# Other groups of experts in a mixture-of-experts block: the first alone, then fours, the last three together; and one expert load three units later

## The chip, the cores and the metric

The kernel runs on one core of a Trainium2 chip. The metric is the device time of one execution in microseconds. Profiles are of one execution; the engines are PE (TensorE matmuls), PEld (its weight loads), DVE (VectorE), ACT (ScalarE), POOL (GpSimd) and SP (SyncE, which here only issues DMAs).

## The reference

512 tokens of width 1024, all float32. A mixer (convolution branch, attention branch, two gates) is followed by a sparse block: each token picks one of 8 groups and two of the group's 8 experts.

```python
u  = rmsnorm(x);  proj = u @ w_in                    # conv B, C, x | q, k, v | two gates
y_conv = (cb * dwconv3(cc * cx)) @ w_conv_out
y_attn = attention(rope(norm(q)), rope(norm(k)), v) @ w_attn_out   # softmax over 512 keys, 8 heads
h  = x + (sigmoid(gc) * y_conv + sigmoid(ga) * y_attn) @ w_o
# experts: g = argmax of 8 group logits, then the top 2 of the 8 experts in g, weights pg * softmax
ys = (silu(xs @ w1[e]) * (xs @ w3[e])) @ w2[e]       # for each of the 64 experts on its tokens
out = h + sum over a token's two experts of weight * ys
```

Each expert has w1 and w3 of 1024x512 and w2 of 512x1024: three arrays of 2 MB, 403 MB for all.

## The kernel before, in words

**The mixer** is a list of units, run in order. A unit is one projection of 128 columns, 24 matmuls (`proj`), with a tile of weights `raw` (0.5 MB) that SP loads one unit ahead. ACT casts `raw` to `wh`, DVE subtracts to get `wl`, the two parts in which a float32 weight is multiplied. `raw`, `wh` and `wl` have two buffers each. PE's outputs are named after the unit: `o_q`, `o_cc`, `o_cx`, `o_cb` while the heads' attention goes on (`s`, `tp_p`, `o_pv`), then `o_g` for the gates and `o_yc` for the convolution's output in turn, eight of each, then `o_g`, `o_ya` and `o_o`. The softmax's rows `p` live in slot `s5`.

**Expert weights** have places of their own: w1 and w3 of expert e in one of three wide slots, used in turn; w2 of expert e in one of four slots named in `order = [5, 2, 6, 7]`. Slot `s5` takes w2 of expert 0. All of these loads are issued by SP, in program order from the gates on (`late`), so a load whose slot is still in use holds up every load behind it in SP's queue. In the profile they are all `w<-in_w`. Nine are issued within the mixer, the others after it, each as soon as its slot is free.

**Experts.** For each expert e (32 places for tokens, `CAP`): `o_x` gathers its tokens by a matmul with a 0/1 matrix `pR`, which DVE transposes into `X`; `h` is its hidden layer (32 steps for w1 and w3 together); ACT and DVE make `gt` from it; `y` is its output, which ACT copies into a quarter of `Y`, 32 rows. Four experts share a `Y`, a matrix `p0` (from `slots_of`, with a row of places for each expert) and its weighted transpose `S`. After the fourth, `combine` spreads all four to the tokens: eight matmuls `o_c` of 128x512, each added to `acc` by DVE. A float32 matmul stands as two records in the trace. The groups are 0 to 3, 4 to 7, and so on to 60 to 63.

**The end.** Of the last group, experts 60 and 61 are spread by `combine_two` (eight `o_c` that read 64 rows), placed between the two halves of `h` of expert 62 and around it. Experts 62 and 63 share two banks for `y`; `last_scatter` makes their matrix `S_last` and the weights `w_last`. `finish_last` first copies half of `acc` into four PSUM banks by an identity matmul (`o_k`), then runs expert 63 and goes through four column pieces: `y` of a piece; ACT and DVE weigh it as two parts `y_last`; eight matmuls spread it into `o_c` (two token tiles) and onto `o_k` (the other two); DVE adds the first to `acc`, ACT copies the second; SP and ACT write the result. The last w2 comes in four pieces.

The order of PE's instructions is that of a scheduler, except where `pin` fixes it. An overflow loop behind the end runs for experts with more than 32 tokens; its instructions stand behind the last store.

Of the kernel before, what the change touches and what calls it, by code (L numbers as in the profile page):

```python
# [46 lines left out]
def block_kernel(ctx, tc, x, norm1_g, w_in, conv_w, q_norm_g, k_norm_g, w_conv_out,  # L47
# [49 lines left out]

    pa, psx, pt = ring((0, 1, 2, 3)), ring((4, 5)), ring((6, 7))

    def mm(o, l, r, start, stop):  # L100
        return TE.matmul(o, l, r, start=start, stop=stop)

    xt = cst.tile([P, NT, D], F32, name="xt")

# [575 lines left out]
        unit(lambda: fn(*args))  # L680

    unit(lambda: late.append(True))
    load_unit(load_output, 0)
    for k in range(NK):
        gate_unit("gc", 2, C_GC, k)
        yc_unit(k)
    for k in range(NK):
        gate_unit("ga", 6, C_GA, k)
        if k in (1, 4):
            load_unit(load_in, 0, k // 4)  # L690
# [199 lines left out]
    def scatter_banks(pwv):  # L890
        tp = pt("tp_s")
        tpv = tp.rearrange("p (k c) -> p k c", k=4)
        for t in range(NT):
            TE.transpose(tpv[:, t, :], pwv[:, t, :], ident)
        return tpv

    def scatter_matrix(pwv):
# [13 lines left out]
    def combine(S, Y, first=False):  # L911
        for t in range(NT):
            for n in range(2):
                combine_at(S, Y, t, n, first)

    def slots_of(posm, gq):
        p0 = mp.tile(shp, F32, tag="p0", name="p0")
        es = slice(4 * gq, 4 * gq + 4)
        for t in range(NT):
            V.tensor_tensor(p0[:, t], posm[:, t, es, None].to_broadcast(shp[:1] + shp[2:]),  # L920
                            io32[:, None, :].to_broadcast(shp[:1] + shp[2:]), op=OP.is_equal)
        return p0

    def weigh(p0, gq):
        es = slice(4 * gq, 4 * gq + 4)
# [10 lines left out]
    def hidden(X, w, meanwhile=None, take=None, between=None):  # L936
        h = (take or psx)("h")
        hv = h[:, 0:2 * P].rearrange("p (i c) -> p i c", i=2)

        for part in (slice(0, 1), slice(1, 2)) if take else (slice(0, 2),):  # L940
            if part.start and between:
                between()
            for k in range(NK):
                for q in range(4):
                    i = mm(hv[32 * q:32 * q + 32, part], X[:, k, :], w[:, part, k, q * P:(q + 1) * P],
                           k == 0, k == NK - 1)
                    if take:
                        pin(i)
        sg = mp.tile([P, P], F32, tag="sg", name="sg", bufs=2)
        A.activation(sg, h[:, 0:P], AF.Silu)  # L950

# [6 lines left out]
        o = meanwhile() if meanwhile else None  # L958
        return gt, o

    def expert(el, X, ws, Y, meanwhile):
        w, c = ws
        gt, o = hidden(X, w, meanwhile=meanwhile)
# [11 lines left out]
    def combine_two(S, Y, ts):  # L975

        for t in ts:
            for n in range(2):
                nsl = slice(n * 512, (n + 1) * 512)
                o = pa("o_c")  # L980
                pin(mm(o, S[:2 * CAP, t, :], Y[:2 * CAP, nsl], True, True))
                V.tensor_tensor(acc_at(t, n), o, acc_at(t, n), op=OP.add)

    def last_scatter():


        p = slot(order[3], [P, NT, 4, CAP], F32, "p_last")
        for t in range(NT):
            for i in range(2):
                e = NE - 2 + i  # L990
                half = [P, 2, CAP]
                V.tensor_tensor(p[:, t, 2 * i:2 * i + 2], posm[:, t, e:e + 1, None].to_broadcast(half),
                                io32[:, None, :].to_broadcast(half), op=OP.is_equal)
        pv = p.rearrange("p t e s -> p t (e s)")
        S = wide_slot((NE - 1) % 3, [P, NT, P], F32R, "S_last")
        A.copy(S, scatter_banks(pv))
        o = pt("w_last")
        for t in range(NT):
            mm(o[:, 0:2], pv[:, t, :], W[:, t, NE - 2:NE], t == 0, t == NT - 1)
        ws = mp.tile([P, 1], F32, name="w_last")  # L1000
        for i in range(2):
            A.copy(ws[64 * i:64 * i + 64, :], o[64 * i:64 * i + 64, i:i + 1])
        return S, ws

    PIECES = list(zip(CUTS, CUTS[1:]))

    def last_two(i, gt, c, y, qs):

        for q in qs:
            c0, c1 = PIECES[q]  # L1010
            for k in range(4):
                r = 64 * i + 32 * (k % 2)
                pin(mm(y[q // 2][r:r + 32, 256 * (q % 2):256 * (q % 2) + 256], gt[:, k * CAP:(k + 1) * CAP], c[k][:, c0:c1],
                       k < 2, k > 1))

    def finish_last(X, ws, y, Sl, wl):

        w, c = ws
        kept = [bank(q, "o_k") for q in range(4)]
        for q, (c0, c1) in enumerate(PIECES):  # L1020
            pin(mm(kept[q].rearrange("p (t c) -> p t c", t=2), ident, acc[:, 2:4, c0:c1], True, False))
        gt, _ = hidden(X, w, take=lambda nm: bank(7, nm))
        hl = slot(order[0], [P, 4, 2, 256], F32R, "y_last")
        ov = out.rearrange("(t p) d -> p t d", p=P)

        def out_of(q):
            last_two(1, gt, c, y, (q,))
            yq = y[q // 2][:, 256 * (q % 2):256 * (q % 2) + 256]
            pin(A.activation(hl[:, q, 0, :], yq, AF.Copy, scale=wl))
            pin(V.scalar_tensor_tensor(hl[:, q, 1, :], yq, wl, hl[:, q, 0, :].bitcast(F32), op0=OP.mult, op1=OP.subtract))  # L1030

        def spread(q):
            c0, c1 = PIECES[q]
            o = bank(6 + q % 2, "o_c")
            for t in range(NT):
                d = (o if t < 2 else kept[q])[:, 256 * (t % 2):256 * (t % 2) + 256]
                pin(mm(d, Sl[:, t, :], hl[:, q, 0, :], t < 2, False))
                pin(mm(d, Sl[:, t, :], hl[:, q, 1, :], False, t != 2))
            for h, src in enumerate((o, kept[q])):
# [65 lines left out]
    for e in range(NE):  # L1105
        if e >= 3:
            load_hidden(e)
            for i in [e + 2] if e < NE - 5 else [e] if e > NE - 4 else []:
                load_output(i)
        if e == 0:  # L1110
            X = X0
        elif e % 4 == 0:
            S = scatter_matrix(weigh(p0, e // 4))
        elif e % 4 == 3 and e < NE - 1:
            p0 = slots_of(posm, e // 4 + 1)
            gathers = prepare_gather(p0, G)
        if e % 4 == 0:
            Y = mp.tile([P, D], F32, tag="Y", name="Y", bufs=2)
        ws = w13.pop(e), wout.pop(e)
        if e == NE - 1:  # L1120
            finish_last(X, ws, y2, Sl, wl)
            break
        if e == NE - 2:

            combine_two(S, Y, (0,))
            gt, _ = hidden(X, ws[0], take=lambda nm: bank(7, nm), between=lambda: combine_two(S, Y, (1,)))
            X = gathered(gathers[3]())
            combine_two(S, Y, (2, 3))
            y2 = [bank(4 + i, "y") for i in range(2)]
            last_two(0, gt, ws[1], y2, range(4))  # L1130
            continue
        X = expert(e % 4, X, ws, Y, gathers[(e + 1) % 4] if e else None)
        if e == NE - 3:
            Sl, wl = last_scatter()
        if e == 0:
            posm, W = finish_routing()
            p0 = slots_of(posm, 0)
            gathers = prepare_gather(p0, V)
            X = gathered(gathers[1]())
            S = scatter_matrix(weigh(p0, 0))  # L1140
        if e == 3:
            acc = mp.tile([P, NT, D], F32, tag="acc", name="acc")
        if e % 4 == 3:
            combine(S, Y, e == 3)
        if e == 7:
            ov_base, ov_tab = overflow_table()
    overflow((wide_slot(0, [P, 2, NK, FE], F32, "ov13"), slot(order[1], [P, 4, D], F32, "ov2")))


# [30 lines left out]
```

## Time and profile before

| | us |
|---|---|
| runs: median (lowest to highest) of 3 | 1464.15 (1463.63 to 1465.65) |
| the profiled execution | 1464.65 |
| its span, first to last instruction | 1462.9 |
| PE busy | 1202.2 (82%) |
| DVE busy | 478.3 (33%) |
| ACT busy | 345.9 (24%) |
| POOL busy | 82.6 (6%) |
| DMA moved | 449.20 MB, 426 GB/s in the slices in which it is full |

Busy times are sums over the span; matmuls overlap, so a busy PE is not PE at its peak. In the page's slices a digit is the busy share of a fortieth of the span in tenths. The chain of waits is followed back from the last instruction: each piece is the work that the next one waited for. A DMA's "time to landing" runs from its issue to the last byte's signal.

### The profile page before, as it was taken

How to read it: one execution, taken by the hardware profiler on the slowest of the kernel's cores; microseconds unless marked ns; L12 is line 12 of the kernel's file. 1: busy time of each engine (PE TensorE's matmuls, PEld its weight loads, DVE VectorE, ACT ScalarE, POOL GpSimd, SP SyncE). 2: the span in 40 equal slices, each digit the busy share in tenths (PEclk: the TensorE clock that was granted, in tenths of full speed). 3: DMA queues.
4: the chain of work that ended last, by engine and by line, in shares of the span. 5: the costliest groups of instructions: out<-in, count | busy, mean ns of one | idle time of the engine just before them, and what ended most of it. 6: DMA issues, size and time to landing. Idle time of an engine off the chain costs nothing.

```text
span 1462.9 us, 25305 instructions
## 1 busy us (share of the span) xinstructions
PE 1202.2 (82%) x11186; PEld 797.2 (54%) x11186; DVE 478.3 (33%) x945; ACT 345.9 (24%) x715; POOL 82.6 (6%) x124
## 2 busy tenths in 40 slices
PE   9999999999999989687585775866857759577597
PEld 7888888778888866343342343433423334343354
DVE  5666665522234343122131221321202212122032
ACT  4444443422232242111111111111111111111121
POOL 1200000000002010000000000000000000000000
PEclk9999999999999999899898998988989899899799
DMA  6222222233645659999999999999999999999994
GB/s 167 76 82 64 68 73 73 93 105 90 208 153 180 265 224 425 426 426 426 427 424 427 426 427 426 426 425 426 426 426 425 427 424 426 428 425 426 426 415 153
DMA packets 110593, 449.20 MB, mean 307 GB/s; under 512 B 11537, under 2 KB 84241, under 8 KB 86034
## 3 DMA queue, kind: packets, MB, share of 16 engines
q1 hardware_dynamic: 110208, 447.29, 75.8%
q8 instruction: 89, 1.46, 0.4%
q10 hardware_dynamic: 274, 0.27, 0.1%
q14 instruction: 22, 0.18, 0.0%
HBM read 445.44 MB, written 2.10 MB: 306 GB/s over the span
## 4 chain that ended last, share of the span: by engine, by line
PE 63%; DMA 31%; ACT 2%; issue 1%; DVE 1%; SPq 1%; POOL 0%; POOLq 0%; ACTq 0%
DMA w<-in_w 31%; PE h L61 11%; PE o_c L61 8%; PE o_g L61 6%; PE y L61 5%; PE o_x L61 3%; PE o_yc L61 3%; PE o_cc L61 3%; PE o_q L61 3%; PE o_cb L61 3%; PE o_ya L61 3%; PE o_o L61 3%; PE o_cx L61 3%; PE s L61 2%; PE o_pv L61 1%
## 5 line engine op out<-in xcount | busy, mean ns | idle before, releaser
L61 PE MATMUL h<-w,X 128*32 128x256 f32 (+1 forms) x4224 | 296.4, 438 | 167.3 <-DMA w<-in_w 166.3
L61 PEld LDWEIGHTS h<-w,X 128*32 128x32 f32 x4224 | 163.5, 127 | 288.8 <-issue 234.7
L61 PE MATMUL y<-w,gt 128*32 128x256 f32 x2048 | 127.7, 381 | 61.4 <-issue 39.9
L61 DVE TENSOR_TENSOR wl<-raw,wh 128x1024 fp32r<-128x1024 f32 x76 | 99.6, 1310 | 132.9 <-ACT wh L61 128.2
L61 PE MATMUL o_x<-xt,pR 128*32 128x256 f32 x2048 | 133.3, 380 | 2.2 <-DVE pR L61 2.2
L61 PEld LDWEIGHTS y<-w,gt 128*32 128x32 f32 x2048 | 70.5, 109 | 115.7 <-issue 52.5
L61 DVE STREAM_TRANSPOSE X<-xs 128x256 f32<-128x256 f32 x64 | 28.4, 444 | 319.6 <-PE h L61 237.5
L61 ACT COPY Y<-y 32x256 f32<-32x256 f32 x248 | 89.9, 363 | 176.7 <-PE y L61 174.4
L61 ACT CAST wh<-raw 128x1024 fp32r<-128x1024 f32 x76 | 80.6, 1060 | 200.3 <-PE o_g L61 64.4
L61 PE MATMUL o_c<-Y,S 128*128 128x512 f32 (+1 forms) x256 | 114.9, 600 | 12.9 <-ACT Y L61 12.9
L61 ACT ACTIVATE sg<-h 128x128 f32<-128x128 f32 x64 | 17.7, 277 | 436.0 <-PE h L61 436.0
L61 DVE TENSOR_TENSOR sp<-h,sg 128x128 f32<-128x128 f32 x64 | 23.0, 360 | 273.0 <-ACT sg L61 273.0
L61 DVE TENSOR_TENSOR acc<-o_c,acc 128x512 f32<-128x512 f32 x124 | 85.8, 692 | 80.0 <-PE o_c L61 79.8
L61 PEld LDWEIGHTS o_x<-xt,pR 128*32 128x32 f32 x2048 | 73.1, 110 | 55.3 <-DVE acc L61 9.9
L61 PEld LDWEIGHTS o_c<-Y,S 128*128 128x128 f32 (+1 forms) x256 | 47.0, 189 | 73.4 <-issue 44.6
L61 PE MATMUL o_g<-u,wh 128*128 128x512 f32 x256 | 80.5, 395 | 0.0
L61 POOL TENSOR_TENSOR pR<-p,rstd 128x512 f32<-128x512 f32 x15 | 15.6, 1043 | 714.3 <-PE o_x L61 671.3
L61 PEld LDWEIGHTS o_g<-u,wh 128*128 128x128 f32 x256 | 48.1, 188 | 11.1
L61 PE MATMUL o_g<-u,wl 128*128 128x512 f32 x128 | 50.5, 394 | 0.0
L61 PE MATMUL o_o<-wh,m 128*128 128x512 f32 x128 | 40.8, 399 | 0.0
L61 PE MATMUL o_q<-u,wh 128*128 128x512 f32 x128 | 40.3, 396 | 0.0
L61 PE MATMUL o_cc<-u,wh 128*128 128x512 f32 x128 | 40.2, 395 | 0.0
(229 smaller groups left out, 1432.4 us busy)
## 6 DMA issues: line engine op xcount, KB each, us to landing
w<-in_w SPq DMA_DIRECT2D x191, 2048.0 KB, 29.4
raw<-in_w_in SPq DMA_DIRECT2D x52, 512.0 KB, 3.8
raw<-in_w_conv_out SPq DMA_DIRECT2D x8, 512.0 KB, 4.1
raw<-in_w_attn_out SPq DMA_DIRECT2D x8, 512.0 KB, 4.1
raw<-in_w_o SPq DMA_DIRECT2D x8, 512.0 KB, 4.8
xt<-in_x SPq DMA_DIRECT2D x4, 512.0 KB, 6.3
w<-in_w SPq DMA_DIRECT2D x4, 512.0 KB, 30.5
out<-acc SPq DMA_DIRECT2D x7, 256.0 KB, 2.3
```

The costliest lines, as they stand in the source:

```text
L61: i = call(*args, **kwargs)
```

## The change

Two things are edited. In the mixer, the load of expert 0's w2 moves from ahead of the first gate to behind the third pair of gate and convolution output. In the experts, the groups become: expert 0 alone, with a matrix of its own (`slots_first`) and a spreading of its own at expert 4 (`combine_first`); 1 to 4, 5 to 8, up to 57 to 60; and 61 to 63, which are spread together at the end. `combine_two` and `last_two` go.

```diff
     unit(lambda: late.append(True))
-    load_unit(load_output, 0)
     for k in range(NK):
         gate_unit("gc", 2, C_GC, k)
         yc_unit(k)
+        if k == 2:
+            load_unit(load_output, 0)
```

Groups: the matrix of group `gq` starts at expert 4 gq + 1; the last has experts 61, 62, 63, 63.

```diff
-        es = slice(4 * gq, 4 * gq + 4)
+        e0, strips = 4 * gq + 1, [slice(0, 4)] if gq < NE // 4 - 1 else [slice(0, 3), slice(2, 3)]
...
+    def combine_first(p, Y):
+        tp = pt("tp_s").rearrange("p (k c) -> p k c", k=4)
+        for t in range(NT):
+            TE.transpose(tp[:CAP, t, :], p[:, t, :], ident)
+        S = mp.tile([P, NT, P], F32, tag="S", name="S", bufs=1)
+        A.copy(S[:CAP], tp[:CAP])
+        for t in range(NT):
             for n in range(2):
                 o = pa("o_c")
-                pin(mm(o, S[:2 * CAP, t, :], Y[:2 * CAP, nsl], True, True))
+                mm(o, S[:CAP, t, :], Y[:CAP, n * 512:(n + 1) * 512], True, True)
                 V.tensor_tensor(acc_at(t, n), o, acc_at(t, n), op=OP.add)
```

The end: 61 and 62 are weighed in one piece beside expert 63's hidden layer, and only the last column piece keeps its `o_k`; in the other three DVE adds both halves. From expert 60 on PE's order is fixed as written (`tail`), and `h` of 62 and 63 is done in two halves, w1 and then w3 (`apart`).

```diff
+    def times_weight(hl, rows_, qs, src, wl):
+        A.activation(hl[rows_, qs, 0, :], src, AF.Copy, scale=wl[rows_])
+        V.scalar_tensor_tensor(hl[rows_, qs, 1, :], src, wl[rows_], hl[rows_, qs, 0, :].bitcast(F32),
+                               op0=OP.mult, op1=OP.subtract)
...
-        kept = [bank(q, "o_k") for q in range(4)]
-        for q, (c0, c1) in enumerate(PIECES):
-            pin(mm(kept[q].rearrange("p (t c) -> p t c", t=2), ident, acc[:, 2:4, c0:c1], True, False))
-        gt, _ = hidden(X, w, take=lambda nm: bank(7, nm))
+        times_weight(hl, slice(0, 64), slice(0, 4), Y[0:64].rearrange("p (q c) -> p q c", q=4), wl)
+        kept = bank(0, "o_k")
+        mm(kept.rearrange("p (t c) -> p t c", t=2), ident, acc[:, 2:4, PIECES[3][0]:], True, False)
+        gt, _ = hidden(X, w, take=lambda nm: bank(5, nm), apart=True)
...
-                if h:
-                    pin(A.copy(d, sv))
+                if h and q == 3:
+                    A.copy(d, sv)
                 else:
-                    pin(V.tensor_tensor(d, sv, d, op=OP.add))
+                    V.tensor_tensor(d, sv, d, op=OP.add)
```

How the instructions stand. First SP's queue where the convolution's output units begin; `raw<-in_w_in` are the projections and gates, `w_0` is w2 of expert 0 (the number behind a name counts tiles), and the lines of the difference are marked - for before and + for now.

```order
 L61 DMA raw<-in_w_in 128x8x128 x33
-L61 DMA w_0_2396<-in_w 128x4096
 L61 DMA raw<-in_w_conv_out 128x8x128
 L61 DMA raw<-in_w_in 128x8x128
...
 L61 DMA raw<-in_w_conv_out 128x8x128
 L61 DMA raw<-in_w_in 128x8x128
+L61 DMA w_0_2589<-in_w 128x4096
 L61 DMA raw<-in_w_conv_out 128x8x128
```

The load goes past six raw loads. On ACT, at the same place, the casts of those raw tiles:

```order
 L61 ACTIVATE p,m<-s,m,r 128x512 x2
+L61 CAST wh<-raw 128x1024
 L61 CAST cbH<-f 128x512
 L61 CAST O<-o_pv 128x512
 L61 CAST pp<-tp_p 128x4x128 x4
 L61 CAST O<-o_pv 128x512
+L61 CAST wh<-raw 128x1024
 L61 ACT_TABLE_LOAD
 L61 ACTIVATE gc<-o_g 128x512
-L61 CAST wh<-raw 128x1024 x4
+L61 CAST wh<-raw 128x1024 x2
```

Two casts that stood behind the first gate now stand ahead of it, the first of them ahead of `cbH`. PE's order in the mixer is the same in both kernels.

PE at experts 3 to 5, before:

```order
L61 MATMUL y<-w_3_3831,gt 32x256 x16
L61 MATMUL tp_s<-identr,p_4241 128x128 x4
L61 MATMUL o_c<-Y,S 128x512 x8
L61 MATMUL h<-w_4_4355,X 32x256 x32
L61 MATMUL o_x<-xt,pR 32x256 x16
L61 MATMUL y<-w_4_3829,gt 32x256 x16
L61 MATMUL o_x<-xt,pR 32x256 x41
L61 MATMUL h<-w_5_4454,X 32x256 x32
```

and now:

```order
L61 MATMUL y<-w_3_3831,gt 32x256 x16
L61 MATMUL o_x<-xt,pR 32x256 x13
L61 MATMUL h<-w_4_4328,X 32x256 x32
L61 MATMUL o_x<-xt,pR 32x256 x3
L61 MATMUL tp_s<-identr,p_first 32x128 x4
L61 MATMUL tp_s<-identr,p_4333 128x128 x4
L61 MATMUL y<-w_4_3829,gt 32x256 x16
L61 MATMUL o_c<-Y,S 128x512 x16
L61 MATMUL h<-w_5_4477,X 32x256 x32
```

The eight `o_c` ahead of `h` of expert 4 are gone, and sixteen stand ahead of `h` of expert 5. PE at the end, from expert 59's `y`, before:

```order
L61 MATMUL y<-w_59_9573,gt 32x256 x16
L61 MATMUL o_c<-Y,S 128x512 x8
L61 MATMUL h<-w_60_9860,X 32x256 x32
...
L61 MATMUL y<-w_61_9960,gt 32x256 x16
L61 MATMUL o_c<-Y,S 128x512 x2
...
L61 MATMUL o_c<-Y,S 128x512 x3
L61 MATMUL h<-w_62_10068,X 32x128 x32
L61 MATMUL o_c<-Y,S 128x512
L61 MATMUL y<-w_62_10071,gt 32x256 x16
L61 MATMUL o_k<-acc,identr 128x512 x4
L61 MATMUL h<-w_63_10208,X 32x128 x64
```

and now:

```order
L61 MATMUL y<-w_59_9596,gt 32x256 x16
L61 MATMUL h<-w_60_9864,X 32x256 x32
L61 MATMUL o_x<-xt,pR 32x256 x16
L61 MATMUL y<-w_60_9695,gt 32x256 x16
L61 MATMUL o_c<-Y,S 128x512 x8
L61 MATMUL h<-w_61_9984,X 32x256 x32
...
L61 MATMUL h<-w_62_10089,X 32x128 x64
L61 MATMUL o_x<-xt,pR 32x256 x16
L61 MATMUL y<-w_62_10092,gt 32x256 x16
L61 MATMUL o_k<-acc,identr 128x512
L61 MATMUL h<-w_63_10208,X 32x128 x64
```

The full `o_c` moved behind `y` of expert 60; the eight `o_c` of `combine_two` and three `o_k` are gone from between `y` of 60 and `h` of 63.

More of the change, by code (lines that the diff above doesn't have):

```diff
@@ L98, in block_kernel @@
     pa, psx, pt = ring((0, 1, 2, 3)), ring((4, 5)), ring((6, 7))
+    tail = []
     def mm(o, l, r, start, stop):
-        return TE.matmul(o, l, r, start=start, stop=stop)
+        i = TE.matmul(o, l, r, start=start, stop=stop)
+        return pin(i) if tail else i
     xt = cst.tile([P, NT, D], F32, name="xt")
@@ L893, in scatter_banks @@
         for t in range(NT):
-            TE.transpose(tpv[:, t, :], pwv[:, t, :], ident)
+            i = TE.transpose(tpv[:, t, :], pwv[:, t, :], ident)
+            if tail:
+                pin(i)
         return tpv
@@ L917, in slots_of @@
         p0 = mp.tile(shp, F32, tag="p0", name="p0")
-        es = slice(4 * gq, 4 * gq + 4)
+        e0, strips = 4 * gq + 1, [slice(0, 4)] if gq < NE // 4 - 1 else [slice(0, 3), slice(2, 3)]
         for t in range(NT):
-            V.tensor_tensor(p0[:, t], posm[:, t, es, None].to_broadcast(shp[:1] + shp[2:]),
-                            io32[:, None, :].to_broadcast(shp[:1] + shp[2:]), op=OP.is_equal)
+            for i, st in enumerate(strips):
+                some = [P, st.stop - st.start, CAP]
+                V.tensor_tensor(p0[:, t, st.start + i:st.stop + i],
+                                posm[:, t, e0 + st.start:e0 + st.stop, None].to_broadcast(some),
+                                io32[:, None, :].to_broadcast(some), op=OP.is_equal)
         return p0
     def weigh(p0, gq):
-        es = slice(4 * gq, 4 * gq + 4)
+        es = slice(4 * gq + 1, 4 * gq + 5)
         for t in range(NT):
@@ L934, in prepare_gather, with hidden @@
         return [lambda el=el: gather_expert(pR[:, :, el * CAP:(el + 1) * CAP]) for el in range(4)]
-    def hidden(X, w, meanwhile=None, take=None, between=None):
+    def hidden(X, w, meanwhile=None, take=None, apart=False):
         h = (take or psx)("h")
         hv = h[:, 0:2 * P].rearrange("p (i c) -> p i c", i=2)
-        for part in (slice(0, 1), slice(1, 2)) if take else (slice(0, 2),):
-            if part.start and between:
-                between()
+        for part in (slice(0, 1), slice(1, 2)) if apart else (slice(0, 2),):
             for k in range(NK):
                 for q in range(4):
[L945 to L948, printed above, removed]
+                    mm(hv[32 * q:32 * q + 32, part], X[:, k, :], w[:, part, k, q * P:(q + 1) * P],
+                       k == 0, k == NK - 1)
         sg = mp.tile([P, P], F32, tag="sg", name="sg", bufs=2)
@@ L959, in hidden, with expert @@
         return gt, o
-    def expert(el, X, ws, Y, meanwhile):
+    def expert(el, X, ws, Y, meanwhile, apart=False):
         w, c = ws
-        gt, o = hidden(X, w, meanwhile=meanwhile)
+        gt, o = hidden(X, w, meanwhile=meanwhile, apart=apart)
         X = gathered(o) if meanwhile else None
@@ L973, in expert, with slots_first, last_scatter @@
         return X
-    def combine_two(S, Y, ts):
-        for t in ts:
+    def slots_first():
+        p = mp.tile([P, NT, CAP], F32, tag="pR", name="p_first", bufs=2)
+        some = [P, NT, CAP]
+        V.tensor_tensor(p, posm[:, :, 0:1].to_broadcast(some), io32[:, None, :].to_broadcast(some), op=OP.is_equal)
+        G.tensor_tensor(p, p, W[:, :, 0:1].to_broadcast(some), op=OP.mult)
+        return p
+    def combine_first(p, Y):
[5 more added lines that the diff above has]
+        for t in range(NT):
             for n in range(2):
-                nsl = slice(n * 512, (n + 1) * 512)
                 o = pa("o_c")
-                pin(mm(o, S[:2 * CAP, t, :], Y[:2 * CAP, nsl], True, True))
+                mm(o, S[:CAP, t, :], Y[:CAP, n * 512:(n + 1) * 512], True, True)
                 V.tensor_tensor(acc_at(t, n), o, acc_at(t, n), op=OP.add)
[L984 to L994, printed above, removed]
+    def last_scatter(p0):
+        pv = p0.rearrange("p t e s -> p t (e s)")
         S = wide_slot((NE - 1) % 3, [P, NT, P], F32R, "S_last")
@@ L998, in last_scatter @@
         for t in range(NT):
-            mm(o[:, 0:2], pv[:, t, :], W[:, t, NE - 2:NE], t == 0, t == NT - 1)
+            mm(o[:, 0:3], pv[:, t, :], W[:, t, NE - 3:NE], t == 0, t == NT - 1)
         ws = mp.tile([P, 1], F32, name="w_last")
-        for i in range(2):
-            A.copy(ws[64 * i:64 * i + 64, :], o[64 * i:64 * i + 64, i:i + 1])
+        for i in range(4):
+            j = min(i, 2)
+            A.copy(ws[32 * i:32 * i + 32, :], o[32 * i:32 * i + 32, j:j + 1])
         return S, ws
@@ L1005, in block_kernel @@
     PIECES = list(zip(CUTS, CUTS[1:]))
[L1007 to L1016, printed above, removed]
+    def times_weight(hl, rows_, qs, src, wl):
+        A.activation(hl[rows_, qs, 0, :], src, AF.Copy, scale=wl[rows_])
+        V.scalar_tensor_tensor(hl[rows_, qs, 1, :], src, wl[rows_], hl[rows_, qs, 0, :].bitcast(F32),
+                               op0=OP.mult, op1=OP.subtract)
@@ L1018, in finish_last @@
+    def finish_last(X, ws, Y, Sl, wl):
         w, c = ws
-        kept = [bank(q, "o_k") for q in range(4)]
-        for q, (c0, c1) in enumerate(PIECES):
-            pin(mm(kept[q].rearrange("p (t c) -> p t c", t=2), ident, acc[:, 2:4, c0:c1], True, False))
-        gt, _ = hidden(X, w, take=lambda nm: bank(7, nm))
         hl = slot(order[0], [P, 4, 2, 256], F32R, "y_last")
+        times_weight(hl, slice(0, 64), slice(0, 4), Y[0:64].rearrange("p (q c) -> p q c", q=4), wl)
+        kept = bank(0, "o_k")
+        mm(kept.rearrange("p (t c) -> p t c", t=2), ident, acc[:, 2:4, PIECES[3][0]:], True, False)
+        gt, _ = hidden(X, w, take=lambda nm: bank(5, nm), apart=True)
+        y = [bank(3 + i, "y") for i in range(2)]
@@ L1024, in finish_last @@
         ov = out.rearrange("(t p) d -> p t d", p=P)
         def out_of(q):
-            last_two(1, gt, c, y, (q,))
+            c0, c1 = PIECES[q]
             yq = y[q // 2][:, 256 * (q % 2):256 * (q % 2) + 256]
-            pin(A.activation(hl[:, q, 0, :], yq, AF.Copy, scale=wl))
-            pin(V.scalar_tensor_tensor(hl[:, q, 1, :], yq, wl, hl[:, q, 0, :].bitcast(F32), op0=OP.mult, op1=OP.subtract))
+            for k in range(4):
+                r = 64 + 32 * (k % 2)
+                mm(yq[r:r + 32], gt[:, k * CAP:(k + 1) * CAP], c[k][:, c0:c1], k < 2, k > 1)
@@ L1032, in spread @@
+            times_weight(hl, slice(64, 128), q, yq[64:128], wl)
         def spread(q):
@@ L1034, in spread @@
             o = bank(6 + q % 2, "o_c")
+            o2 = kept if q == 3 else bank(1 + q % 2, "o_c")
             for t in range(NT):
[L1036 to L1039, printed above, removed]
+                d = (o if t < 2 else o2)[:, 256 * (t % 2):256 * (t % 2) + 256]
+                mm(d, Sl[:, t, :], hl[:, q, 0, :], t < 2 or q < 3, False)
+                mm(d, Sl[:, t, :], hl[:, q, 1, :], False, t != 2 or q < 3)
+            for h, src in enumerate((o, o2)):
                 d = acc[:, 2 * h:2 * h + 2, c0:c1]
                 sv = src.rearrange("p (t c) -> p t c", t=2)
-                if h:
-                    pin(A.copy(d, sv))
+                if h and q == 3:
+                    A.copy(d, sv)
                 else:
-                    pin(V.tensor_tensor(d, sv, d, op=OP.add))
+                    V.tensor_tensor(d, sv, d, op=OP.add)
                 (A if h and q == 3 else SP).dma_start(ov[:, 2 * h:2 * h + 2, c0:c1], d)
@@ L1109, in block_kernel @@
                 load_output(i)
+        el = (e - 1) % 4
         if e == 0:
             X = X0
-        elif e % 4 == 0:
+        elif el == 0 and 1 < e < NE - 3:
             S = scatter_matrix(weigh(p0, e // 4))
-        elif e % 4 == 3 and e < NE - 1:
-            p0 = slots_of(posm, e // 4 + 1)
+        elif el == 3:
+            p0 = slots_of(posm, e // 4)
             gathers = prepare_gather(p0, G)
-        if e % 4 == 0:
+        if e == 0 or el == 0:
             Y = mp.tile([P, D], F32, tag="Y", name="Y", bufs=2)
+        if e == NE - 4:
+            tail.append(True)
         ws = w13.pop(e), wout.pop(e)
         if e == NE - 1:
-            finish_last(X, ws, y2, Sl, wl)
+            finish_last(X, ws, Y, Sl, wl)
             break
[L1123 to L1132, printed above, removed]
+        X = expert(el if e else 0, X, ws, Y, gathers[e % 4] if e else None, apart=e == NE - 2)
         if e == NE - 3:
-            Sl, wl = last_scatter()
+            Sl, wl = last_scatter(p0)
         if e == 0:
+            Y0 = Y
             posm, W = finish_routing()
@@ L1138, in block_kernel @@
             gathers = prepare_gather(p0, V)
-            X = gathered(gathers[1]())
+            X = gathered(gathers[0]())
             S = scatter_matrix(weigh(p0, 0))
+        if e == 2:
+            p_first = slots_first()
         if e == 3:
             acc = mp.tile([P, NT, D], F32, tag="acc", name="acc")
-        if e % 4 == 3:
-            combine(S, Y, e == 3)
+        if e and el == 3:
+            combine(S, Y, e == 4)
+        if e == 4:
+            combine_first(p_first, Y0)
         if e == 7:
             ov_base, ov_tab = overflow_table()
+    tail.clear()
     overflow((wide_slot(0, [P, 2, NK, FE], F32, "ov13"), slot(order[1], [P, 4, D], F32, "ov2")))
```

## The prediction

> **What bounds the kernel now.** The first thing to read is the page's slices, since the shares of the whole span mix two stages.
>
> ```profile
> PE   9999999999999989687585775866857759577597
> ...
> DMA  6222222233645659999999999999999999999994
> ```
>
> Each digit is 36.6 us. Up to slice 15 PE is full and the DMA mostly idle: the mixer is bound by TensorE. From slice 16 the DMA is full until the last slice and PE is not: the experts are bound by the stream of their weights. So a microsecond counts in three places only: in the mixer on PE's path (it moves the start of the stream), inside the stream if it runs dry, and behind its end. The chain of waits shows the first:
>
> ```profile
> 282.07 1.68 ACT pp L61 x4
> 283.75 9.06 DMA raw<-in_w_conv_out
> ...
> 295.20 6.93 PE o_yc L61 x22
> 302.13 5.57 PE o_g L61 x24
> ...
> 318.86 5.58 PE o_yc L61 x24
> ...
> 380.21 44.61 PE o_g L61 x192
> 424.83 44.63 PE o_ya L61 x192
> 469.46 42.34 PE o_o L61 x181
> ```
>
> Columns are start, length, what. A DMA of the mixer's weights is on the chain for 9.06 us; everything from 302 to 512 is PE without a break. The stream's first load behind the mixer waits for the last o_o, so what is saved at 283 is saved at the stream's start. PE's timeline at this place, with the idle time before an instruction in brackets:
>
> ```profile
> 291.43 0.40 PE L61 MATMUL o_g<-u,wl 128*128 128x512 f32 x1
> 293.94 0.50 PE L61 MATMUL o_yc<-cbH,wh 128*128 128x512 f32 x1 [2.11 <-ACT wh L61]
> ...
> 295.20 0.75 PE L61 MATMUL o_yc<-cbH,wl 128*128 128x512 f32 x1 [0.53 <-DVE wl L61]
> ```
>
> SP's waits and issues there say who is late:
>
> ```profile
> SPq L61 <- DVE p L61: 19.8, 1, 19.8
> ```
> ```profile
> 283.32 0.34 SPq L61 DMA_DIRECT2D w<-in_w  x1
> ...
> 304.28 0.37 SPq L61 DMA_DIRECT2D raw<-in_w_conv_out  x1
> ```
>
> SP stands up to 19.8 us at expert 0's output weights, whose slot the softmax still uses. Two mixer loads, the first of w_conv_out and the one of the second gate, stand behind it in the same queue; the first is issued at 283.75, when the chain's DMA begins.
>
> **The front, step by step.** Without the wait the first o_yc would follow the last o_g at the pace of 5.57 / 24 = 0.23 us, at 291.66, and take 5.58 as the later ones do; the next o_g would start at 297.24. It starts at 302.13: 4.9 us are lost. Part of that is clock:
>
> ```profile
> 295.29:298.70 3.41, 3.41 (x8) 2.68 (x9) 1.23 (x1) 0.22 (x1) 0.00 (x0) 0.50 0.56 161
> ```
>
> After the idle window PE got clock 0.50 for 3.41 us (eight matmuls, where the next window holds sixteen). The change sends the two mixer loads ahead of expert 0's load. Their buffers come free with the conversions of the units before, the first one's by the time at which SP's long wait begins, so it is converted while PE works on o_cb and o_g (ACT's order has this cast before cbH), and the second one has the 5.58 us of the first o_yc to spare. The gain is 4.9; the low end is 0, if the same stall comes back at the new place. There the load has no slot to wait for, since p was read by 283, but 2 MB go ahead of the next raw load. The nearest row is a load of the same kind with a raw load behind it:
>
> ```profile
> 426.97 0.37 SPq L61 DMA_DIRECT2D raw<-in_w_attn_out  x1
> ```
> ```profile
> DMA to landing us min/median/max: 7.3/7.3/7.3
> ```
> ```profile
> raw<-in_w_in SPq DMA_DIRECT2D x52, 512.0 KB, 3.8
> ```
>
> It landed after 7.3 instead of 3.8 us, and o_ya ran its 44.63 us unbroken. In the gate stage a raw load is issued at 304.28 for the o_yc at 318.86, 14.6 us ahead; 7.3 plus the 2.4 from a landing (283.75 + 9.06) over cast and subtraction to 295.20 fits. I take the whole 4.9. [...]
>
> **The tail.** The chain's end:
>
> ```profile
> 1396.28 7.13 PE o_c L61 x16
> 1403.41 3.59 PE h L61 x64
> ...
> 1437.25 3.63 PE o_k L61 x8
> 1440.88 3.68 PE h L61 x128
> ...
> 1445.66 1.08 PE y L61 x8
> ...
> 1448.92 0.67 PE o_c L61 x4
> 1449.59 0.47 PE o_k L61 x4
> ```
>
> From 1396 PE never waits long, yet the last expert's weights are there earlier than it comes to them. The issues of its two hidden-layer loads and their times to landing:
>
> ```profile
> L61 SPq DMA_DIRECT2D w<-in_w x1: 327/327/327, 1407.1 to 1407.1; - x1
> ...
> DMA to landing us min/median/max: 24.9/24.9/24.9
> ```
> ```profile
> L61 SPq DMA_DIRECT2D w<-in_w x1: 433/433/433, 1407.4 to 1407.4; - x1
> ...
> DMA to landing us min/median/max: 29.5/29.5/29.5
> ```
>
> So w1 of expert 63 lands at 1432.0 and w3 at 1436.9, while h63 runs from 1440.88 to 1444.56. The change takes PE work from between:
>
> ```profile
> L61 PE MATMUL o_c<-Y,S 64*128 64x512 f32 x16 | 7.9, 615 | 0.9 <-ACT Y L61 0.9
> ```
>
> These 16 records (eight matmuls that spread experts 60 and 61) vanish; the full-height o_c of the row at 1396.28, 7.13 us, moves from before h60 to after y60 and stays; three of the four o_k go, 2.7 us. With 7.1 for the o_c, PE comes to h63 about 9.8 us earlier, at 1431.1, and then waits for the weights: the gain is cut by them. The first half of h63 can run at 1432.0, the second at 1437.0. A half measured
>
> ```profile
> 1430.50 1.96 PE L61 MATMUL h<-w,X 128*32 128x128 f32 x64
> ```
>
> so h63 ends at 1438.9 at full clock, 5.6 us earlier. But PE now idles there about 1 us before the first half and 3 between the halves, and more if the other steps are quicker. The price of idling is in the row of a window around an earlier h that waited 5 us:
>
> ```profile
> 1384.14:1390.96 6.82, 4.52 (x44) 2.49 (x48) 0.00 (x0) 0.00 (x0) 0.00 (x0) 0.50 1.00 425
> ```
>
> 44 records in 4.52 us at clock 0.50 are 103 ns each, against 3.59/64 = 56 at full clock. A half of h63 at that pace takes 3.5: it ends at 1440.5, 4.1 us earlier. I take 4.0 since three idle microseconds are like the 2.6 at 292 to 295 that brought a 0.50 window. The four pieces behind h63 keep their PE work (y, eight matmuls of spreading). DVE gets one more addition in each of the first three pieces:
>
> ```profile
> 1454.16 1.49 DVE L61 TENSOR_TENSOR acc<-o_c,acc 128x512 f32<-128x512 f32 x2
> ```
> ```profile
> 1455.44 0.58 ACT acc L61
> ```
>
> The first two fit into DVE's gaps; the third puts the last addition's end at 1454.16 + 3 x 0.7 = 1456.3 instead of 1455.65, beside ACT's last copy that ends at 1456.02. I charge 0.5. The weighing of experts 61 and 62 in one piece (64x1024 on ACT and on DVE) runs while PE waits for w1 and w3, and costs nothing; if that cover were gone it would stand ahead of the last expert's Silu on the same two engines. Behind h63's waits stand only the pieces, whose w2 parts land after w3 in the same stream and before they are used. Sum of the tail: 4.0 - 0.5 = 3.5, between 0 and 5.6.
>
> **The rest of the change.** Expert 0's own spreading adds eight matmuls, four small transposes and eight additions at expert 4. That is 7.13 us more PE work where the stream binds:
>
> ```profile
> 580.26 1.77 PE y L61 x32
> ...
> 583.33 27.22 DMA w<-in_w
> ```
> ```profile
> 591.70 1.93 PE L61 MATMUL y<-w,gt 128*32 128x256 f32 x32 [0.47 <-issue]
> ```
>
> Loads already issued keep the DMA busy until 610.55. What frees the next slot is y5, at 593.6 now. With twice 7.13 us of o_c behind y4 (which starts at 580.26 - 7.13 = 573.1, since no o_c stands before h4, and ends at 575), a wait of 1 for Y, then h 3.6, o_x and y of 1.9 each, y5 ends near 597.7: 4 us later, 12.8 before the stream would run dry. Cost 0. Groups that start at expert 1 instead of 0 shift the o_c by one expert in a stream that repeats; cost 0, covered by the 29 us that the loads are issued ahead:
>
> ```profile
> w<-in_w SPq DMA_DIRECT2D x191, 2048.0 KB, 29.4
> ```
>
> **Sum.** The profiled execution took 1464.65 (span 1462.9), 0.5 above the median of the runs, 1464.15. 1464.65 - 4.9 - 3.5 = 1456.25, or 1455.8 on the median's footing.
>
> **Rivals.**
> First, the clock eats the tail. PE idles up to 6 us of the 8 before h63's second half, and if the 0.50 windows reach over the pieces behind it, each piece's PE work of 1.08 + 0.67 + 0.47 = 2.2 us grows by the ratio 103/56 to 4.1: up to 7.4 over four, more than the 5.6 at stake. A tail gain of 0 gives 1459.3, the worst, 7.4 - 5.6 = 1.8 lost, 1461.1. For it: 295.29. Against: one busy window restored the clock there. Chance 0.13. [...]
> Second, only the tail gains: the stall at 292 returns at the next raw load behind expert 0's weights: 1464.15 - 3.5 = 1460.6. Chance 0.08.
> Third, slower: the stream runs dry behind expert 4. It decides when y5 ends later than 610; from there each microsecond costs one. If the whole block of 21.7 us ran at half clock, y5 would end near 619, and with some 2 us until the DMA is full again 11 would be lost: 1467. Against: the 12.8 us of room. Chance 0.05.
> Fourth, no effect: PE does not reach h63 earlier, and the mixer's saving is lost in the routing ahead of expert 0: 1464. Chance 0.04.
>
> **Numbers.** The forecast, both gains, has 0.70 and spans 1453.0 (4.9 + 5.6, less half a microsecond for the scatter of runs) to 1458.6. The range to 1460.8 takes in the second rival and most of the first. 0.2% is 2.9 us, about what a measurement of this kernel can tell from no change, so faster means below 1461.2: 0.70 + 0.12 + 0.07 = 0.89; same 0.06; slower 0.05.
>
> **What the new profile would show.** The DMA of w_conv_out is off the chain at 283, o_yc follows o_g with no wait and no 0.50 window, and the second o_g starts near 297.2. The last load of the stream lands about 4.9 earlier. PE waits for w<-in_w before each half of h63, and h63 ends 9 us earlier than now (4.9 + 4.0). DVE ends the last addition 0.5 after ACT's copy rather than before it. I am wrong if PE waits in the gate stage elsewhere, if DMA digits below 9 show near 600, or if the last pieces run at clock 0.50.

## The result, and the profile after

The changed kernel takes 1456.8 us (median of 5 runs, 1454.37 to 1457.07) against 1464.74 for the kernel before beside it; the ratio is 0.9942 [0.9928, 0.9957], 7.9 us less. The forecast was 1455.8 within 1453.0 to 1460.8. The profiled execution is the fastest of the five, 1454.37 us (span 1452.6): 10.3 below the profiled one of before, so 2.4 of what the two profiles differ by is scatter. The page's slices of the changed kernel:

```profile
PE   9999999999999989986775957768577586775785
PEclk9999999999999999898989989989899897997998
DMA  6222222243645669999999999999999999999995
```

The two stages are as before: PE full to slice 15, the DMA full behind it. The chain of waits of the changed kernel (start, length, what) in the stage of the gates:

```profile
281.44 1.75 PE tp_p L61 x16
...
288.24 3.49 PE o_g L61 x15
291.73 5.57 PE o_yc L61 x24
297.31 5.57 PE o_g L61 x24
302.88 5.58 PE o_yc L61 x24
...
464.63 42.19 PE o_o L61 x181
```

The DMA of w_conv_out is off the chain, the second o_g starts at 297.31 instead of 302.13, and o_o 4.83 earlier than the 469.46 of before. A window in the old stall's place has the clock at 1.00:

```profile
294.87:298.30 3.43, 3.43 (x16) 2.78 (x15) 0.80 (x2) 1.05 (x1) 0.00 (x0) 1.00 0.53 153
```

The end of the same chain:

```profile
1391.34 3.69 PE h L61 x64
...
1395.42 36.61 DMA w<-in_w
1432.07 2.00 PE h L61 x64
...
1435.18 1.08 PE y L61 x8
...
1437.33 1.06 PE y L61 x8
1438.39 1.14 PE o_c L61 x8
...
1444.95 0.68 DVE acc L61
```

Where PE's o_c, h and o_k stood in a row, a load now stands: the last w3, which lands at 1395.42 + 36.61 = 1432.03, against 1407.4 + 29.5 = 1436.9 before. That is the front's gain arriving at the end of the stream. From this landing to the end of the execution it takes 1454.37 - 1432.03 = 22.3 us, and took 27.7: the tail's 5.4. PE's timeline there, with the idle time before an instruction in brackets:

```profile
1427.20 3.33 PE L61 MATMUL h<-w,X 128*32 128x128 f32 x64 [2.92 <-DMA w<-in_w]
1432.07 1.96 PE L61 MATMUL h<-w,X 128*32 128x128 f32 x64 [1.54 <-DMA w<-in_w]
...
1437.33 1.06 PE L61 MATMUL y<-w,gt 128*32 128x256 f32 x8 [1.09 <-DVE y_last L61]
```

PE waits for the weights before each half of expert 63's h. The first half took 3.33 us, the second 1.96, and the windows around them (start:end, length, then busy time of each engine, granted clock, DMA share, GB/s) say why:

```profile
1426.67:1430.09 3.42, 2.89 (x56) 2.92 (x60) 0.59 (x1) 0.00 (x0) 0.00 (x0) 0.50 0.94 352
1430.09:1433.50 3.41, 1.87 (x68) 1.60 (x64) 0.00 (x0) 0.00 (x0) 0.00 (x0) 1.00 0.54 172
```

One window at clock 0.50 fell on the first half. That half was done at 1430.5, before the last w3 landed at 1432.03, so it cost nothing; the half that the end hangs on ran at full clock.

### The profile page after: what moved, and what is told of

Read it like the earlier page. It is cut to its first block, busy times and chain, and to the rows that moved or that the text cites. A ratio compares the mean times of both kernels' runs of the same rounds, so it can differ in the third digit from the quotient of the medians.

```text
span 1452.6 us, 25294 instructions
## 1 busy us (share of the span) xinstructions
PE 1199.1 (83%) x11180; PEld 796.6 (55%) x11180; DVE 482.7 (33%) x946; ACT 346.9 (24%) x719; POOL 80.5 (6%) x121
## 4 chain that ended last, share of the span: by engine, by line
PE 62%; DMA 31%; issue 2%; DVE 2%; ACT 2%; SPq 1%; POOL 0%; DVEq 0%; POOLq 0%; ACTq 0%
DMA w<-in_w 31%; PE h L61 11%; PE o_c L61 8%; PE o_g L61 6%; PE y L61 5%; PE o_x L61 4%; PE o_cc L61 3%; PE o_q L61 3%; PE o_cb L61 3%; PE o_ya L61 3%; PE o_cx L61 3%; PE o_yc L61 3%; PE o_o L61 3%; PE s L61 2%; PE o_pv L61 2%
## 5 line engine op out<-in xcount | busy, mean ns | idle before, releaser
L61 PE MATMUL o_c<-Y,S 128*128 128x512 f32 (+1 forms) x256 | 118.1, 615 | 13.3 <-ACT Y L61 12.6
```

Of the source, the lines that this page charges most:

```text
L61: i = call(*args, **kwargs)
```

## The experiments

Times are medians with their lowest and highest; ratios are to runs of the kernel before on the same chip, whose medians were 1464.3 to 1464.9.

**The two parts.** First the load's move alone, in the kernel before:

```diff
-    load_unit(load_output, 0)
     for k in range(NK):
...
+        if k == 2:
+            load_unit(load_output, 0)
```

> The kernel before with only expert 0's load moved. By the step of the prediction: 4.9 us less than before, 1459.8; no wait and no 0.50 window at the first o_yc, the first load behind the mixer issued 4.9 earlier, the tail as before. By the rival (the stall moves to the next raw load behind the 2 MB): no change, 1464.7, with a wait of PE in the gate stage near 310.

1459.84 us (1459.16 to 1460.21), ratio 0.997 [0.9959, 0.9981]: 4.4 less. The first load behind the mixer is issued at 517.40, as in the changed kernel. Then the groups alone, with the load at its old place:

```diff
+    load_unit(load_output, 0)
     for k in range(NK):
...
-        if k == 2:
-            load_unit(load_output, 0)
```

> The changed kernel with expert 0's load back ahead of the first gate: only the groups of experts are changed. If the two parts add up: 7.9 less 4.9, so 3.0 us less than before, 1461.7 (1459.3 if the clock falls as in the first profile of the changed kernel). If the clock eats the tail: 1464 to 1465. If the parts do not add up, the stream is the reason, and the last load lands elsewhere than before.

1460.12 us (1458.51 to 1461.68), 0.9973 [0.9963, 0.9983]: 4.2 less, more than expected, with a wide interval (2.5 to 5.4). The last w3 landed at 1436.18 in its profile, 0.7 earlier than before, so most of the gain lies behind the stream. The sum of both parts, 8.6, stands beside 7.9 for the whole and 6.7 in a second set of its runs (below; interval 5.0 to 9.1): the parts add up within the scatter, and neither needs the other.

**Whether the load's new place matters.** Behind the first pair, at k == 0, instead of the third:

```diff
-        if k == 2:
+        if k == 0:
             load_unit(load_output, 0)
```

> The changed kernel with expert 0's load behind the first pair of gate and convolution output instead of the third: two raw loads stand ahead of it and one that is wanted at 303 stands behind it. If what cost 4.9 us was only that loads stood behind a wait for the slot, any place at which the load no longer waits long does: same as the changed kernel, 1457, with w_conv_out's second tile landing near 292 and cast in time. If the 2 MB ahead in the queue are what costs, PE waits at the second o_yc for 2 to 5 us: 1459 to 1462.

1456.88 us (1456.78 to 1458.69), 0.9949 [0.9935, 0.9963]: that of the changed kernel. SP's queue, the time from issue to landing of the raw load behind the 2 MB, and the chain:

```profile
283.56 0.34 SPq L61 DMA_DIRECT2D w<-in_w  x1
284.00 0.39 SPq L61 DMA_DIRECT2D raw<-in_w_conv_out  x1
```
```profile
DMA to landing us min/median/max: 9.0/9.0/9.0
```
```profile
292.07 5.57 PE o_yc L61 x24
297.65 5.57 PE o_g L61 x24
303.22 5.58 PE o_yc L61 x24
```

The raw load still takes 9.0 us behind expert 0's weights, but it is the one for the o_yc at 303.22, 10 us after its landing at 293. So 2 MB ahead of a raw load cost nothing here; what the place before cost was that the first two raw loads stood behind SP's wait. The queue alone does not explain the 4.9 us, though. Before, the first tile's cast also stood on ACT behind the first gate's sigmoid `gc`, which waits for that gate's o_g:

```profile
291.87 0.60 ACT L61 ACTIVATE gc<-o_g 128x512 f32<-128x512 f32 x1 [1.60 <-PE o_g L61]
292.84 1.04 ACT L61 CAST wh<-raw 128x1024 fp32r<-128x1024 f32 x1 [0.38 <-DMA raw<-in_w_conv_out]
```

The cast waited only 0.38 us more for the load, so in that order of ACT an earlier landing would have bought about 0.4 us (an estimate from these two rows). The load's new place changed both, SP's queue and the cast's place on ACT; no run changes one without the other.

**The clock in the tail.** The changed kernel again, for a second profile:

> The changed kernel once more. Its profiled execution took 1454.37 us while the other four took 1456.67 to 1457.07, so the question is which of the two comes back. Theory A (the tail's clock): the 2.4 us lie behind the stream's end, where PE idles before each half of expert 63's h and the 0.50 windows fall differently from run to run; a new profile that is near 1456.8 then shows 0.50 over the second half of h or over the pieces of y, and w3 of expert 63 landing at about 1432.0 as in the first profile. Theory B (the stream): w3 of expert 63 lands about 2.4 us later, and the tail behind it has the same length.

1457.57 us (1455.43 to 1457.96), 0.9952 [0.9938, 0.9966]; profiled at 1457.84. The last w3 lands at 1432.29, 0.26 later than in the first profile; the end comes 3.5 later. PE's timeline and two windows:

```profile
1427.41 2.48 PE L61 MATMUL h<-w,X 128*32 128x128 f32 x64 [2.90 <-DMA w<-in_w]
1432.33 3.48 PE L61 MATMUL h<-w,X 128*32 128x128 f32 x64 [2.44 <-DMA w<-in_w]
...
1439.13 1.92 PE L61 MATMUL y<-w,gt 128*32 128x256 f32 x8 [1.09 <-DVE y_last L61]
```
```profile
1428.70:1435.50 6.80, 4.36 (x86) 3.69 (x80) 0.00 (x0) 0.00 (x0) 0.00 (x0) 0.50 0.64 213
1438.90:1442.30 3.40, 3.17 (x14) 1.88 (x15) 0.72 (x3) 0.47 (x1) 0.00 (x0) 0.50 0.02 5
```

The windows lie 2 us later in the program, and now the half-clock ones cover the second half of h (3.48 for 1.96) and the second piece (y 1.92 for 1.06, its o_c 1.83 for 1.22): 1.5 + 0.9 + 0.6 and the 0.26 of the landing are 3.3 of the 3.5. The program and its waits are the same; the windows lie elsewhere. To take the waits out of PE's sight, eleven matmuls of 128x128 whose result nobody reads go before each half:

```diff
         for part in (slice(0, 1), slice(1, 2)) if apart else (slice(0, 2),):
+            if between:
+                between(11 if part.start else 11)
...
+        def fill_in(n):
+            for _ in range(n):
+                mm(idle[:, 0:P], ident, xt[:, 0, 0:P], True, True)
```

> The changed kernel with eleven 128x128 matmuls into an unused bank ahead of each half of expert 63's h, about 2.4 us each, where PE waits for w1 and w3. Theory A: PE keeps clock 1.00 through the end, and all runs come out near 1454, 2.5 us under the changed kernel's median. Theory B: 1456.8 as before, the same spread. If the added matmuls are longer than the waits they put off h and cost up to 1 us.

1454.6 us (1454.21 to 1456.83), 0.9936 [0.9922, 0.995]: 2.2 to 3.0 below the two medians of the changed kernel. The profiled run is the highest; in it h stood still for 0.85 us in the middle of its second half, which waits for nothing that the profile shows, and one window of 0.50 came over the second piece (its y took 1.92 us for 1.06; the mean clock from 1423 to 1447 is 0.93, about 3.4 of the 24 us at 0.50). The cause of that stop is open. The second cure is for the pause of 1.09 us between the pieces: y of pieces 0 and 1 share a bank, and the second one waits for DVE's `y_last`, which reads the first (1.09 <-DVE y_last in both profiles).

```diff
-            yq = y[q // 2][:, 256 * (q % 2):256 * (q % 2) + 256]
+            yq = y[q % 2][:, 256 * (q // 2):256 * (q // 2) + 256]
```

> The changed kernel with the four pieces of y in alternate banks: piece 1 no longer shares its bank with piece 0, so its matmuls need not wait for DVE's reading of piece 0 (1.09 us in the profile). Expected: 1.0 us less in each run, 1456, and fewer 0.50 windows over the pieces, since one of the two pauses of 1.1 us is gone; if the 0.50 windows come from the waits for w1 and w3 alone, exactly 1.0.

1454.87 us (1454.46 to 1455.46), 0.9933 [0.9919, 0.9946]: 1.9 to 2.7 less, twice or more what was expected. The pause itself is 1.1 us, and it is gone: y of pieces 0 and 1 stand below as one row of sixteen records, 1.92 us. The rest is not shown run by run, but it fits the clock: in this profile no window of 0.50 fell on the pieces, although the second half of h took 3.35 us for the 1.96 of full clock:

```profile
1432.12 3.35 PE L61 MATMUL h<-w,X 128*32 128x128 f32 x64 [2.15 <-DMA w<-in_w]
1436.63 1.92 PE L61 MATMUL y<-w,gt 128*32 128x256 f32 x16 [1.16 <-DVE gt L61]
```

Both cures in one kernel:

> Both: the added matmuls ahead of each half of expert 63's h, and the pieces of y in alternate banks. By the theory of the clock no 0.50 window is left before the end, and the runs come out between 1453.0 and 1454.0, closer together than those of the changed kernel. By the other theory 1.0 less than the changed kernel, 1456.

1453.21 us (1452.81 to 1453.4), 0.9921 [0.9907, 0.9934], the fastest kernel of the case: 11.4 below the kernel before, 3.6 to 4.4 below the changed one, and the runs lie within 0.6 us instead of 3.6 (ten runs of the changed kernel). Both halves of h run at full clock (1.00 in each of five windows from 1423.2 to 1440.2):

```profile
1426.78 1.95 PE L61 MATMUL h<-w,X 128*32 128x128 f32 x64
...
1431.64 2.11 PE L61 MATMUL h<-w,X 128*32 128x128 f32 x64 [0.25 <-DMA w<-in_w]
```

**Expert 4.** The prediction had y of expert 5 ending at 597.7 by the old kernel's times, which is 592.8 with the front's 4.9 taken off. It ended at 601.5. PE's timeline of the changed kernel:

```profile
570.05 1.93 PE L61 MATMUL y<-w,gt 128*32 128x256 f32 x32 [0.22 <-issue]
572.82 7.13 PE L61 MATMUL o_c<-Y,S 128*128 128x512 f32 x16 [0.84 <-ACT Y L61]
580.62 11.13 PE L61 MATMUL o_c<-Y,S 32*128 32x512 f32 x16 [0.67 <-ACT S L61]
591.68 6.38 PE L61 MATMUL h<-w,X 128*32 128x256 f32 x64
...
599.61 1.90 PE L61 MATMUL y<-w,gt 128*32 128x256 f32 x32
```
```profile
583.58:597.24 13.66, 13.66 (x65) 5.20 (x67) 4.07 (x6) 0.59 (x1) 0.00 (x0) 0.50 1.00 425
```

PE is busy for all of these 13.66 us, and has clock 0.50 throughout. The difference between the two sets of o_c is the number of rows that they read, 128 or 32. So expert 0's were made to read 128, of which 96 are zero:

```diff
+        for r in (slice(32, 64), slice(64, 128)):
+            G.memset(S[r], 0.0)
...
-                mm(o, S[:CAP, t, :], Y[:CAP, n * 512:(n + 1) * 512], True, True)
+                mm(o, S[:, t, :], Y[:, n * 512:(n + 1) * 512], True, True)
...
+            for r in (slice(32, 64), slice(64, 128)):
+                G.memset(Y0[r], 0.0)
```

> The changed kernel with expert 0's o_c reading all 128 rows, 96 of which are zero in both operands, instead of 32. In the profile of the changed kernel PE is busy without a pause at these sixteen records and yet gets clock 0.50 from 583.6 on. Theory C: matmuls over 32 rows count too little as activity. Then clock 1.00 stays through them here, they take about 7.1 us instead of 11.1, and y of expert 5 ends about 8 us earlier. Theory D: the clock fell for the pauses of 0.84 and 0.67 us ahead of the o_c. Then the 0.50 windows stay. The total time is the same by both within 1 us, since the stream does not run dry there.

1456.14 us (1455.07 to 1456.37), 0.9939 [0.9924, 0.9954]. The o_c took 7.13 us, the h behind them 3.66, and the same stretch has clock 1.00:

```profile
580.00 7.13 PE L61 MATMUL o_c<-Y,S 128*128 128x512 f32 x16
587.07 3.66 PE L61 MATMUL h<-w,X 128*32 128x256 f32 x64
```
```profile
583.58:597.24 13.66, 13.66 (x198) 7.43 (x200) 5.86 (x11) 3.07 (x8) 0.00 (x0) 1.00 1.01 428
```

With 64 rows, 32 of them zero, one profiled run:

```diff
+        G.memset(S[CAP:2 * CAP], 0.0)
...
-                mm(o, S[:CAP, t, :], Y[:CAP, n * 512:(n + 1) * 512], True, True)
+                mm(o, S[:2 * CAP, t, :], Y[:2 * CAP, n * 512:(n + 1) * 512], True, True)
...
+            G.memset(Y0[CAP:2 * CAP], 0.0)
```

> The changed kernel, with expert 0's eight products reading 64 rows, of which 32 are zero; between the changed kernel (32 rows: 11.13 us, clock 0.50 from 583.6 to 597.2) and the one with 128 rows (7.13 us, clock 1.00 throughout). Theory (the clock counts used rows, and 64 of 128 are enough, as in the 64-row products of the kernel before, whose mean was 615 ns in clock 1.00): the products take about 7.1 us, no window of 0.50 between 580 and 600, y of expert 5 ends near 594. Rival (half the rows leave the clock undecided or at half): one or more windows of 0.50 and 8 to 11 us. The total stays at 1454 to 1458 either way.

1458.55 us, and at expert 4 the same picture:

```profile
581.80 7.13 PE L61 MATMUL o_c<-Y,S 64*128 64x512 f32 x16 [0.72 <-POOL S L61]
```
```profile
583.40:597.20 13.80, 13.80 (x169) 7.14 (x171) 6.67 (x12) 2.36 (x7) 0.00 (x0) 1.00 1.01 429
```

(In its tail the second half of h took 3.50 us and the second piece 1.92, as in the second profile of the changed kernel.) In these runs reading 32 rows is what halved the clock, and 64 were enough to keep it. A set of eight products on 32 rows took 11.13 us, and 11.5 and 12.2 on average in the two kernels below that repeat it; with 64 or 128 rows it took 7.13 in all three profiles (the third is the kernel with all three edits, below). The pauses of Theory D are out: with 64 rows they are still there, 0.84 and 0.72 us, and the clock stays at 1.00. y of expert 5 ended at 594.2 with 128 rows and at 596.0 with 64, 7.3 and 5.5 earlier than in the first profile of the changed kernel, but the end of the program comes no earlier beyond the scatter: 1456.14 and 1458.55, against medians of 1456.8 and 1457.57. What expert 4 lost is hidden. How much more would be hidden was asked by issuing each of expert 0's products two and three times (the extra ones write the same sums again; `range(3)` in the second kernel):

```diff
-                mm(o, S[:CAP, t, :], Y[:CAP, n * 512:(n + 1) * 512], True, True)
+                for _ in range(2):
+                    mm(o, S[:CAP, t, :], Y[:CAP, n * 512:(n + 1) * 512], True, True)
```

> The eight products of combine_first are each issued twice (the second writes the same sums again); nothing else differs from the changed kernel. Theory (expert 4's block has a margin of some 4 to 9 us before the stream of weights runs dry, because y of expert 5 releases the next w2 load): the eight extra products run at clock 0.50 for at least their greater part (11.1 us, at most 7.1 us if at full clock), y of expert 5 ends at 601.5 + 11 = about 612 instead of 601.5, the load behind it is issued about 6 us after the stream's last queued load has landed (605.7), the DMA shows a gap there, and the end comes 2 to 9 us later than the changed kernel's 1456.8: 1459 to 1466. Rival (the stream is not held by this block, since w1/w3 loads issued earlier carry it on): the end is the same, 1456 to 1458, and the DMA stays full through 590 to 625.

> The same, each product issued three times. Theory: y of expert 5 ends some 18 to 22 us later than in the changed kernel (about 620 to 623), so the loss grows with a slope of 1 over what the doubled kernel shows: 7 to 11 us more than that kernel, 1468 to 1477. Rival: the same time as the changed kernel.

Twice: 1466.9 us (1463.33 to 1468.57), ratio 1.0014 [1.0005, 1.0024], 2.0 slower than the kernel before. Three times: 1480.11 (1479.33 to 1481.96), 1.0111 [1.0094, 1.0128]. The DMA's busy tenths from 560 to 640, in steps of 2 us, in the changed kernel, then with two and with three times the products:

```profile
DMA  9999999999999999999999999999999999999999
```
```profile
DMA  9999999999999999999997100669999999999999
```
```profile
DMA  9999999999999999999996000000000006999999
```

and SP's issues of the loads that wait for y of expert 5, in the same order:

```profile
601.58 1.28 SPq L61 DMA_DIRECT2D w<-in_w  x3
```
```profile
610.54 1.28 SPq L61 DMA_DIRECT2D w<-in_w  x3
```
```profile
625.89 1.28 SPq L61 DMA_DIRECT2D w<-in_w  x3
```

The last load that was queued before them lands at 605.66, 605.92 and 605.52. From 560 to 640 the DMA moved 33.92, 30.49 and 23.77 MB; at the 424 GB/s of the changed kernel the 3.43 and 10.15 MB less are 8.1 and 23.9 us of the stream, for issues that came 9.0 and 24.3 us later. So the first 0.9 or 0.4 us were free and from there each microsecond cost one: by the rows of 2 us above the DMA is full again 2 to 3.5 us after an issue, and the changed kernel issues 4.1 us before the last queued load lands. Its room is about one microsecond. The expected loss of the doubled kernel, 2 to 9, was exceeded slightly by the medians (10.1); 8.1 of it is the gap in the stream, and where the other 2.0 went is not shown. The tripled one lies 13.2 above it, where 7 to 11 was expected: its third set took 13.8 us at half clock and the h behind them 6.39 against 4.82.

All three edits that help PE's clock, in one kernel:

> The changed kernel with all three edits: expert 0's products on 128 rows, fillers before each half of h of expert 63, the pieces' y in alternate banks. The 128 rows gave no gain in the total by themselves, since the stream isn't held by expert 4. Theory: the same as the kernel with the two tail edits, 1452.8 to 1453.4 (1452 to 1454 with scatter), and tight. Rival (half the clock at expert 4 costs something now hidden by the tail's scatter): below 1452.

1453.57 us (1453.17 to 1454.38), 0.9923 [0.9906, 0.9939], no faster than with the two tail edits. The half clock at expert 4 costs this kernel nothing. The products on 128 rows (or 64) give back room, with y of expert 5 ending at 594 to 596 instead of 601.5, but no time.

## Why the prediction was right, and where it was not

**The front** was worked out as 4.9: the next o_g at 297.24, and it started at 297.31; 4.83 at o_o, 4.98 at the first load behind the mixer (517.38 for 522.36), 4.4 by the medians of the load alone. The second rival, that the stall comes back behind the 2 MB, is out by the kernel that gave it the best chance (the load behind the first pair): the raw load took 9.0 us behind the 2 MB, where 4.1 is the median of the eight loads of w_conv_out, and PE never saw it. The step left out that the first tile's cast stood behind `gc` on ACT before the change: it was right that the cast moves ahead, and by the two rows of ACT above, which is an estimate, that move was needed too.

**The tail** was taken as 4.0 less 0.5, between 0 and 5.6. The steps came as written: both waits for weights are there, and h63 ends at 1434.0, 10.5 earlier than before (4.9 + 5.6, the full-clock end) in the first profile; in the second at 1435.8, 8.7 earlier (4.9 + 3.8, the half-clock end). Over both medians of the changed kernel (1456.8 and 1457.57, 7.9 and 6.7 less than the kernel before beside each) the tail gave 3.0 and 1.8 beside a front of 4.9, by the groups alone 4.2. The first rival's mechanism is therefore part of the likeliest case rather than an alternative to it: the half clock reached one piece of the four in the second profile and cost 1.5 there, not the 7.4 over all four that the rival priced, and not nothing. A last piece at clock 0.50 was one of the signs of being wrong that the prediction had named; it appeared, at a fifth of the rival's price. The program does not fix where the windows lie: in the two profiles they are 2 us apart at the same instructions (0.50 from 1426.67 in the first and from 1428.70 in the second).

**The additions on DVE** were charged at 0.5. The last one ends at 1444.95 + 0.68 = 1445.63, ACT's last copy at 1445.48: it costs 0.15. The weighing of experts 61 and 62 costs nothing, as said; it ran on ACT from 1424.80 and on DVE from 1425.98 for 1.28 us, under PE's wait for w1.

**The step that was mis-sized is expert 4's**, and it was luck that it did no harm: one microsecond was left. The working took 7.13 us for the eight products on 32 rows and 3.6 for the h behind them, from rows at full clock; they took 11.13 and 6.38, and y of expert 4 started 1.9 later than placed: 4.0 + 2.8 + 1.9 = 8.7, the whole of the miss. The room was given as 12.8, with no time for the DMA to start; the third rival's price put "some 2 us" on that start without a row for it, and it took 2 to 3.5. Measured, the room is about 1, and the third rival's mechanism appears in full as soon as the products are doubled. Its chance of 0.05 rested on the 12.8 us and on the full clock, and neither was there.

## What to carry to other kernels

A load that waits for its buffer holds up what is queued behind it, here two raw loads behind a wait of 19.8 us: ask for each load whether its buffer is free when its turn comes, and put it behind the loads whose buffers are. Look also at where the work on the late tile stands on its own engine, since that order may hold the stall by itself (by the estimate above all but 0.4 us of it). Where PE must wait for the last transfers, give it work that nobody reads and remove the short pauses of about a microsecond behind them; this bought 3.6 to 4.4 us here and took away most of the scatter. Before a block is called hidden, measure from the last queued transfer back how late its release may come, since a margin worked out at full clock can be gone at half: here 12.8 us were worked out, and about one was there.

## What the runs showed of the hardware that was not expected

- A busy PE was granted half the clock. Products on 32 rows, back to back, ran at 1.00 for their first 3 to 5 us and at 0.50 from there for as long as they lasted; in the kernel with three times the products:

```profile
584.00:615.00 31.00, 31.00 (x38) 11.95 (x36) 4.15 (x6) 0.00 (x0) 0.00 (x0) 0.50 0.63 268
```

In the gate stage of the kernel before, one busy window at 0.50, 295.29 to 298.70, was followed by one at 1.00, to 302.10. Here 31 us, nine times as long, were not, and the clock came back only in the h that follows, whose matmuls read 128 rows: at 597.24 for an h that starts at 591.68 in the changed kernel, at 604.6 for 602.19 with twice the products. With 64 or 128 rows the clock stayed at 1.00 (583.40 to 597.20 and 583.58 to 597.24), although 32 and 96 of these rows hold zeros. So in these runs the rows that a product reads counted, not only whether PE was busy, with the bound between 32 and 64 rows for these float32 products of 512 columns. How the hardware counts them is not shown.
- A window with work in it was followed by half the clock too. Pauses of 2.4 and 2.9 us ahead of the halves of h were followed by 0.50 in the second profile (1428.70 to 1435.50), and so was a window in which PE stood for two pauses of about 1.1 us and was busy for 1.37 of 3.40 us (ahead of the second piece):

```profile
1435.50:1438.90 3.40, 1.37 (x20) 0.40 (x11) 1.00 (x3) 0.75 (x2) 0.00 (x0) 1.00 0.09 30
```

- Ten runs of the changed kernel spread over 3.6 us, and five runs of the one with the waits filled and the pause gone over 0.6. In the profiles what differs is where the clock's windows lie.
